# Gated attention in a one-core decoder block: another column order, level products in halves, value products in quarters

## The chip, the cores and the metric

The kernel runs on one core of a Trainium2 chip. The metric is the device time of one execution in microseconds (us), lower is better. The kernel before takes 565.12 us, the median of three runs (565.05 to 565.92).

In this text PE is the matrix engine (TensorE), PEld its weight loads, DVE the vector engine, ACT the scalar engine, POOL the engine GpSimd, and SP the engine that issues most transfers. A matmul has a stationary operand, loaded first, and a moving operand that streams through it column by column; the profile gives each a record of its own. A product of plain float32 operands appears as two pairs of such records.

## The reference

One decoder layer on 512 tokens of width 1024: RMSNorm, one input projection whose columns go to three head groups, an output projection with a residual, an MLP with squared ReLU, and a final RMSNorm. Group A is dilated attention (6 heads), group C block attention (6 heads), and group B, which the change is mainly about, is gated linear attention with 4 heads, keys of 32 and values of 64 columns:

```python
log_a = jax.nn.log_sigmoid((a_lr @ w_a2 + b_a)) / B_GATE_TAU      # per token and key column
b = jnp.cumsum(log_a)                                             # within a chunk
decay = jnp.exp(where(causal, b_i - b_j, NEG_INF))
attn = jnp.einsum('bhnic,bhnjc,bhnijc->bhnij', qc, kc, decay)
o_intra = jnp.einsum('bhnij,bhnjv->bhniv', attn, vc)
o_inter = jnp.einsum('bhnic,bhncv->bhniv', qc * jnp.exp(b), s_prev)
o = rmsnorm(o_intra + o_inter) * norm_w * silu(r)
```

Groups A and C end in a softmax over scores plus bias, `p = exp(l - max) / sum`, followed by the product with the values.

## The kernel before

**Group B without large exponents.** The tokens are cut into four blocks of 128 (`NB`). Inside a block the causal triangle is split by levels, `LEVELS = (64, 32, 16, 8, 4, 2, 1)`: a pair (query i, key j) belongs to the level L at which i lies in the upper half and j in the lower half of the same group of 2L tokens. `levels` makes for each level one tile `kq` (four heads of 32 key columns on the 128 partitions, 512 tokens along the row) in which the lower halves hold keys and the upper halves hold queries, both scaled by the decay to the middle of the group. The level product of block n and head h is then one matmul: all 128 tokens of the block as the stationary operand, the 64 tokens of the upper halves as the moving one, over the head's 32 partitions. The result, 128 keys by 64 queries, goes to the bank `lp[h]` of PSUM. There are 7 levels, 4 blocks and 4 heads, so 112 matmuls; levels are done in pairs (64 and 32, 16 and 8, 4 and 2, 1), and a pair takes four banks, two of tag `s` and two of tag `pt`. The four heads lie in four strips of 32 rows of the PE.

**Merging.** The results are put together in `attn[h]` (128 keys, 4 blocks, 128 queries; zeroed first by POOL). For L of 64 and 32, ACT copies the rectangles. For L of 16 and less, DVE copies the whole result under the mask `lmask` (`copy_predicated`), 256 elements a row for each of 4 heads; queries stand in their natural order, so that a level writes runs of L elements with gaps of L. A bank is given back after the second level of the pair is merged from it.

**Values.** `carry` makes the states between blocks (`smk`) and the decayed queries (`eq`). Then, block by block, one matmul adds the state's part (`eq` by `smk`, 256 columns, not for block 0), and four add `attn[h]` (128 by 128, stationary) by the head's values (64 columns), into the banks `op_`. DVE adds the diagonal part and the result is normalized and gated.

**Softmax.** `attention` goes through six pairs of heads; for each pair and each of four query blocks it spawns two streams `softmax`, one for each head (`side` e = 0, 1). A stream is: DVE adds the bias and takes the minimum `mn` (signs are turned), ACT takes the exponential and the row sum `z`, DVE takes the reciprocal `rz`, and DVE or ACT, whichever would be done first, scales the row. There are 48 such streams. `turn` then transposes the scaled rows on the PE, and `values` multiplies.

**What sets the order.** Every engine runs its instructions in the order in which they were issued. That order is made by `Plan`, which simulates the engines when the program is built: each piece of work is a stream (a generator), and `Plan.run` always issues the step that could start first by its own clock, with a priority as the tie-break. An operation is booked at the cost that `Op.__init__` gives it, and 0.2 us (`SWITCH`) when the matmul before it had another shape class (32 or 64 rows, 32 or 64 columns of the PE). So a changed cost, or an operation more or less, can change the order of everything issued after it. Most lines of the trace bear line 133, where `issue` makes the instruction; the tiles' names tell the work apart: `lp` level products, `attn` merges, `op` value products, `rz`, `z` and `P` softmax, `sps` scores, `ptp` transposes, `po` products of attention with values, `vps`, `qkps`, `ops`, `f1*`, `f2*` the dense projections, `wh` and `wl` the two parts into which ACT and DVE split each weight.

## Time and profile before

| what | us |
|---|---|
| median of three runs | 565.12 |
| the profiled execution | 566.03 |
| its span, first to last instruction | 564.0 |
| PE busy | 553.6 |
| DVE busy | 479.6 |
| ACT busy | 370.3 |
| POOL busy | 69.0 |

The profiled execution is one of its own: its span is 2.03 us shorter than its time, and its time is 0.91 us above the median of the three runs. A group row gives engine, operation, output and inputs, size and count, then the busy time and the mean length of one in ns. A timeline row gives start, length over all of its merged instructions, engine, operation and count. A window row gives the busy time of PE, PEld, DVE, ACT and POOL with the number of instructions, then the granted PE clock and the transfers' share.

### The profile page before, as it was taken

The numbers are of one execution on the slowest core, as the hardware profiler recorded it, in microseconds if no ns is written. First come the engines' busy times: TensorE is split into PE (matmuls) and PEld (weight loads), VectorE is DVE, ScalarE is ACT, GpSimd is POOL, SyncE is SP. The second block draws the span as 40 slices with busy tenths as digits, with TensorE's granted clock in tenths as the row PEclk, the third lists the DMA queues.
The fourth block names the chain that finished last, engine by engine and source line by source line (L and its number), as shares of the span: only waits on it lengthen the run. The fifth ranks groups of instructions, "written<-read, shape, count | busy, mean of one in ns | idle before, by whom it ended". The sixth has DMA issues, their size and how long they took to land.

```text
span 564.0 us, 9463 instructions
## 1 busy us (share of the span) xinstructions
PE 553.6 (98%) x3513; PEld 477.8 (85%) x3513; DVE 479.6 (85%) x874; ACT 370.3 (66%) x659; POOL 69.0 (12%) x90
## 2 busy tenths in 40 slices
PE   8999999999999999999999999999999999999995
PEld 7977887786876768899987899988999888999884
DVE  5799899978867988999799995799957799867985
ACT  5755744694865775989766476855477655579553
POOL 5003110000010002110111010120020110011103
PEclk9999999999999999999999999999999999999998
DMA  8945594685134765992989429687378594395803
GB/s 301 400 121 118 91 261 95 205 320 112 37 43 121 254 146 112 268 274 60 278 212 209 158 64 279 198 149 206 113 162 279 121 201 160 94 216 113 150 18 131
DMA packets 29948, 96.58 MB, mean 171 GB/s; under 512 B 3648, under 2 KB 3690, under 8 KB 29904
## 3 DMA queue, kind: packets, MB, share of 16 engines
q0 software_dynamic: 9456, 33.53, 33.4%
q1 hardware_dynamic: 20160, 62.20, 30.9%
q8 instruction: 27, 0.44, 0.3%
q10 hardware_dynamic: 288, 0.27, 0.1%
q14 instruction: 17, 0.14, 0.1%
HBM read 93.86 MB, written 2.13 MB: 170 GB/s over the span
## 4 chain that ended last, share of the span: by engine, by line
PE 83%; DVE 9%; DMA 3%; ACT 2%; issue 2%; SPq 0%; DVEq 0%; ACTq 0%; POOLq 0%
PE f2X L133 14%; PE f1X L133 13%; PE qkps L133 10%; PE f1Z L133 8%; PE f2Z L133 7%; PE ops L133 7%; PE vps L133 5%; PE f1Y L133 4%; PE f2Y L133 3%; DMA wraw<-in_w 3%; PE ptp L133 3%; PE po L133 2%; DVE wl L133 2%; PE sps L133 2%; PE av L133 1%
## 5 line engine op out<-in xcount | busy, mean ns | idle before, releaser
L133 DVE TENSOR_TENSOR wl<-wraw,wh 128x1024 fp32r<-128x1024 f32 (+2 forms) x174 | 192.0, 1110 | 39.5 <-ACT wh L133 39.1
L133 ACT ACTIVATE wh<-wraw 128x1024 fp32r<-128x1024 f32 (+2 forms) x173 | 164.6, 966 | 58.1 <-DMA wraw<-in_w 12.3
L133 PE MATMUL f1X<-yp,wh 128*128 128x256 f32 x512 | 92.7, 283 | 0.0
L133 PEld LDWEIGHTS f1X<-yp,wh 128*128 128x128 f32 x512 | 80.1, 192 | 0.3
L133 POOL DMA_DIRECT2D wraw<-in_w x46 | 40.5, 948 | 270.2 <-DVE wl L133 227.2
L133 PE MATMUL f1X<-yp,wl 128*128 128x256 f32 x256 | 72.5, 283 | 0.0
L133 PE MATMUL f2X<-wh,Al 128*128 128x512 f32 (+1 forms) x132 | 50.6, 383 | 0.0
L133 PE MATMUL f2X<-wh,Ah 128*128 128x512 f32 (+1 forms) x132 | 50.6, 383 | 0.0
L133 PE MATMUL f2X<-wl,Ah 128*128 128x512 f32 (+1 forms) x132 | 50.5, 383 | 0.0
L133 PEld LDWEIGHTS f1X<-yp,wl 128*128 128x128 f32 x256 | 49.1, 192 | 0.1
L133 PE MATMUL f1Z<-yp,wh 128*128 128x256 f32 x256 | 46.3, 283 | 0.0
L133 ACT ACTIVATE h<-h 128x512 f32<-128x512 f32 x56 | 34.7, 625 | 10.5 <-DVE h L133 9.9
L133 PE MATMUL qkps<-xh,wh 128*128 128x512 f32 x96 | 40.1, 418 | 0.0
L133 PEld LDWEIGHTS f1Z<-yp,wh 128*128 128x128 f32 x256 | 39.9, 192 | 0.0
L133 ACT ACTIVATE P<-P,mn 128x512 f32<-128x512 f32 (+3 forms) x48 | 26.5, 555 | 18.8 <-DVE mn L133 18.8
L133 ACT ACTIVATE Ah<-h 128x512 fp32r<-128x512 f32 x40 | 24.0, 620 | 21.5 <-DVE h L133 21.5
L133 PE MATMUL qkps<-xh,wl 128*128 128x512 f32 x96 | 37.6, 392 | 0.0
L133 PE MATMUL qkps<-xl,wh 128*128 128x512 f32 x96 | 37.5, 390 | 0.0
L133 PE MATMUL f1Z<-yp,wl 128*128 128x256 f32 x128 | 36.2, 283 | 0.0
L133 DVE TENSOR_TENSOR Al<-h,Ah 128x512 fp32r<-128x512 f32 x40 | 26.9, 686 | 3.2 <-ACT Ah L133 3.1
L133 PEld LDWEIGHTS f2X<-wl,Ah 128*128 128x128 f32 x132 | 24.8, 188 | 4.9
L133 PEld LDWEIGHTS f2X<-wh,Ah 128*128 128x128 f32 x132 | 24.8, 188 | 4.8
(264 smaller groups left out, 1220.8 us busy)
## 6 DMA issues: line engine op xcount, KB each, us to landing
wraw<-in_w SPq DMA_DIRECT2D x66, 512.0 KB, 5.2
wraw<-in_w POOLq DMA_DIRECT2D x46, 512.0 KB, 6.7
wraw<-in_wqk SPq DMA_DIRECT2D x12, 512.0 KB, 6.0
wraw<-in_wv SPq DMA_DIRECT2D x10, 512.0 KB, 6.7
wraw<-in_wv POOLq DMA_DIRECT2D x8, 512.0 KB, 5.4
wraw<-in_wo SPq DMA_DIRECT2D x8, 512.0 KB, 7.1
wraw<-in_wo POOLq DMA_DIRECT2D x8, 512.0 KB, 5.5
nb<-tab SPq DMA_DIRECT2D x12, 256.0 KB, 3.5
```

The source lines that it names most:

```text
L133: getattr(getattr(self.nc, op.eng), op.method)(*op.args, **op.kw)
```

## The change

Five edits, all in the diff. (1) The columns of `lp` and `attn` get another order: query i of a block stands at place 4·(i mod 32) + (i div 32). The mask follows. A level then writes runs of 4L elements. To deliver its columns in that order, the moving operand of a level product is read with a step of 32 tokens in its innermost dimension for all levels but 32. (2) Each level product becomes two, one for keys 0 to 63 and one for keys 64 to 127: 224 matmuls with 64 stationary columns. (3) Each value product becomes four with 32 stationary columns, one for each 32 queries; in `attn` these are every fourth element. The three products with the states come first. (4) Level 16 is merged by ACT in four rectangles a head, no longer by DVE; levels 64 and 32 write other places. (5) The two softmax streams of a pair share a tile `z` of two columns; one of them takes both reciprocals in one operation once both sums are there, so neither row is scaled before that. Beside that the planner books level products at 0.024 us each (0.031 before), float32 products by another formula, and 0.2 us more for a float32 product of 512 columns.

```diff
--- before.py
+++ after.py
@@ -58,9 +58,9 @@
             if method != "matmul":
                 self.cost = 0.109
             elif wide and inner[-1].shape[0] == 32:
-                self.cost = 0.031
+                self.cost = 0.024
             elif wide:
-                self.cost = 0.002 + max(n / 600 / (1 + (args[0].shape[0] == 64)), 0.21)
+                self.cost = 0.002 + max(n / 600, 0.21 if args[0].shape[0] > 64 else 0.132) / {32: 4, 64: 2}.get(args[0].shape[0], 1) + 0.2 * (n == 512 and args[0].shape[0] == 128)
             elif inner[-1].shape[0] == 64:
                 self.cost = max(n / 2260, 0.12) / 2
             else:
@@ -820,25 +820,42 @@
             for i, (li, L) in enumerate(pair):
                 kq = lev.pop(li)
                 for n in range(NB):
-                    for h in range(4):
-                        c = kq[32 * h:32 * h + 32, n * 128:(n + 1) * 128]
-                        o = lp[h][:, i * 256 + n * 64:i * 256 + (n + 1) * 64]
-                        ops.append(PE.matmul(o.rearrange("p (m l) -> p m l", l=L), c,
-                                             c.rearrange("p (m l) -> p m l", l=2 * L)[:, :, L:], start=True, stop=True))
+                    for rows in (slice(0, 64), slice(64, 128)):
+                        for h in range(4):
+                            c = kq[32 * h:32 * h + 32, n * 128:(n + 1) * 128]
+                            o = lp[h][rows, i * 256 + n * 64:i * 256 + (n + 1) * 64]
+                            if L == 32:
+                                o = o.rearrange("p (m l) -> p m l", l=L)
+                                d = c.rearrange("p (m l) -> p m l", l=2 * L)[:, :, L:]
+                            elif L == 64:
+                                o = o.rearrange("p (l k) -> p l k", k=2)
+                                d = c[:, L:].rearrange("p (k l) -> p l k", k=2)
+                            else:
+                                o = o.rearrange("p (m l k) -> p m l k", l=L, k=4)
+                                d = c.rearrange("p (k m l) -> p m l k", k=4, l=2 * L)[:, :, L:]
+                            ops.append(PE.matmul(o, c[:, rows], d, start=True, stop=True))
             yield ops
             for i, (li, L) in enumerate(pair):
                 give("lev")
-                m = 64 // L
-                mk = lmask[:, li, :].rearrange("p (m l) -> p m l", l=L)[:, None, :, :].to_broadcast([128, NB, m, L])
+                m = 16 // L
+                mk = lmask[:, li, :].rearrange("p (m l) -> p m l", l=64 if L > 16 else 4 * L)
                 for h, r in enumerate(("s", "s", "pt", "pt")):
-                    o4 = attn[h].rearrange("p n (m l) -> p n m l", l=2 * L)[:, :, :, L:]
-                    src = lp[h][:, i * 256:i * 256 + 256].rearrange("p (n m l) -> p n m l", n=NB, l=L)
-                    if L >= 32:
-                        for j in range(m):
-                            rows = slice(2 * L * j, 2 * L * j + L)
-                            yield ACT.activation(o4[rows, :, j], src[rows, :, j], AF.Copy)
+                    src = lp[h][:, i * 256:i * 256 + 256].rearrange("p (n c) -> p n c", n=NB)
+                    o4 = attn[h].rearrange("p n (l k) -> p n l k", k=4)
+                    if L == 64:
+                        yield ACT.activation(o4[:64, :, :, 2:], src[:64].rearrange("p n (l k) -> p n l k", k=2), AF.Copy)
+                    elif L == 32:
+                        for j in range(2):
+                            rows = slice(64 * j, 64 * j + 32)
+                            yield ACT.activation(o4[rows, :, :, 2 * j + 1], src[rows, :, 32 * j:32 * j + 32], AF.Copy)
+                    elif L >= 16:
+                        for j in range(4):
+                            rows = slice(32 * j, 32 * j + 16)
+                            yield ACT.activation(o4[rows, :, 16:, j], src[rows].rearrange("p n (l k) -> p n l k", k=4)[:, :, :, j], AF.Copy)
                     else:
-                        yield DVE.copy_predicated(o4, mk, src)
+                        o4 = attn[h].rearrange("p n (m l) -> p n m l", l=8 * L)[:, :, :, 4 * L:]
+                        yield DVE.copy_predicated(o4, mk[:, None, :, :].to_broadcast([128, NB, m, 4 * L]),
+                                                  src.rearrange("p n (m l) -> p n m l", l=4 * L))
                     if li == pair[-1][0]:
                         give(r)
         fire("attn")
@@ -849,13 +866,15 @@
         for i in range(2):
             yield ("take", "pt")
             op_.append(bank("pt", "op"))
+        for n in range(1, NB):
+            ops.append(PE.matmul(op_[n // 2][:, n % 2 * 256:n % 2 * 256 + 256], eq[:, n * 128:(n + 1) * 128], smk[n - 1],
+                                 start=n < 3, stop=False, skip_group_check=True))
         for n in range(NB):
-            o = op_[n // 2][:, n % 2 * 256:n % 2 * 256 + 256]
-            vb = vB[n // 2][:, n % 2, :]
-            if n:
-                ops.append(PE.matmul(o, eq[:, n * 128:(n + 1) * 128], smk[n - 1], start=True, stop=False, skip_group_check=True))
-            ops.extend(PE.matmul(o[:, h * 64:(h + 1) * 64], attn[h][:, n, :], vb[:, h * 64:(h + 1) * 64],
-                                 start=(n == 0 and h == 0), stop=h == 3, skip_group_check=True) for h in range(4))
+            for h in range(4):
+                for k in range(4):
+                    ops.append(PE.matmul(op_[n // 2][32 * k:32 * k + 32, n % 2 * 256 + h * 64:n % 2 * 256 + (h + 1) * 64],
+                                         attn[h][:, n, k::4], vB[n // 2][:, n % 2, h * 64:(h + 1) * 64],
+                                         start=False, stop=h == 3, skip_group_check=True))
         yield ops
         for i in range(2):
             yield DVE.tensor_tensor(oB[i].rearrange("p t c -> p (t c)"), op_[i], dv[i].rearrange("p t c -> p (t c)"), op=OP.add)
@@ -1051,12 +1070,24 @@
                 spawn(mix_out(p if p < 3 else p + 2, po, r), 1)
 
     def softmax(P, s, nb, key, last):
-        mn, z, rz = (small(x, (128, 1)) for x in ("mn", "z", "rz"))
+        mn = small("mn", (128, 1))
+        p, side, qb = key
+        if ("z", p, qb) not in st:
+            st["z", p, qb] = small("z", (128, 2)), small("rz", (128, 2))
+        z, rz = st["z", p, qb]
         yield DVE.tensor_tensor_reduce(P, s, nb, 1.0, 3e38, OP.add, OP.min, mn)
         if last:
             give(last)
-        yield ACT.activation(P, P, AF.Exp, bias=mn, scale=-1.0, accum_out=z)
-        yield DVE.reciprocal(rz, z)
+        yield ACT.activation(P, P, AF.Exp, bias=mn, scale=-1.0, accum_out=z[:, side:side + 1])
+        fire(("z", *key))
+        yield ("wait", ("z", p, 1 - side, qb))
+        if ("z", p, qb) in st:
+            st.pop(("z", p, qb))
+            yield DVE.reciprocal(rz, z)
+            fire(("rz", p, qb))
+        else:
+            yield ("wait", ("rz", p, qb))
+        rz = rz[:, side:side + 1]
         yield Any(DVE.tensor_scalar(P, P, rz, None, op0=OP.mult), ACT.activation(P, P, AF.Copy, scale=rz),
                   late=dict(vector=LN))
         fire(key)
@@ -1718,7 +1749,7 @@
     cst[p, 1024 + p // 32] = 1.0
     lm = np.zeros((128, len(LEVELS), 64), np.int32)
     for li, L in enumerate(LEVELS):
-        i = np.array([x for x in range(128) if x // L % 2 == 1])
+        i = np.array([x for x in np.arange(128).reshape(4, 32).T.flat if x // L % 2 == 1])
         j = np.arange(128)
         lm[:, li, :] = (j[:, None] // L % 2 == 0) & (j[:, None] // (2 * L) == i[None, :] // (2 * L))
     return oh, ind, cst, lm
```

## The prediction

> **What bounds the kernel now.** I read the page's busy line first, then the busy time by stage, then the waits of PE.
>
> ```profile
> PE 553.6 (98%) x3513; PEld 477.8 (85%) x3513; DVE 479.6 (85%) x874; ACT 370.3 (66%) x659; POOL 69.0 (12%) x90
> ...
> core 0: us, PE busy (x) PEld busy (x) DVE busy (x) ACT busy (x) POOL busy (x), PEclk, DMA share, GB/s
> 60.00:70.00 10.00, 10.00 (x106) 8.43 (x105) 8.35 (x20) 8.15 (x19) 1.20 (x2) 1.00 0.46 70
> 70.00:80.00 10.00, 10.00 (x100) 8.27 (x100) 10.00 (x25) 3.22 (x4) 1.61 (x2) 1.00 0.99 265
> 90.00:100.00 10.00, 10.00 (x78) 7.78 (x77) 10.00 (x21) 2.19 (x3) 0.00 (x0) 1.00 0.21 68
> 100.00:110.00 10.00, 9.51 (x63) 7.66 (x63) 10.00 (x40) 7.04 (x20) 0.00 (x0) 1.00 0.54 161
> 300.00:557.00 257.00, 257.00 (x1620) 233.92 (x1618) 217.37 (x272) 159.76 (x221) 32.39 (x35) 1.00 0.63 159
> ...
> 0.00:10.00 10.00, 7.62 (x41) 6.99 (x42) 3.82 (x11) 4.82 (x8) 7.04 (x19) 1.00 0.82 277
> 556.00:564.10 8.10, 1.21 (x11) 1.00 (x9) 3.28 (x14) 2.35 (x5) 0.43 (x1) 0.80 0.35 129
> ```
>
> PE is idle 10.4 us of the span: 2.4 us in the first ten, 6.9 us after 556, and some 1.1 us between. So the time is PE's work plus its fixed ends. DVE is as full as PE from 70 to 110 us, where the gated attention runs; after 300 us PE never idles, and nothing of the change lies there. What PE waits for in between:
>
> ```profile
> PE f2Z L133 <- ACT wh L133: 0.4, 1, 0.4
> PE ptp L133 <- DVE P L133: 0.3, 1, 0.3
> PE sps L133 <- DVE mn L133: 0.2, 1, 0.2
> ```
>
> Time saved on PE is therefore worth its full size; time saved on DVE is worth the half microsecond that `ptp` and `sps` wait for it.
>
> **Level products in halves.** One pair of levels, and the last level:
>
> ```profile
> 56.87 2.01 PE L133 MATMUL lp<-kq 32*128 32x64 f32 x64
> 58.81 0.50 PE L133 MATMUL vps<-wh,xh 128*128 128x512 f32 x1
> ...
> 90.41 1.35 PE L133 MATMUL lp<-kq 32*128 32x64 f32 x32
> 91.69 0.50 PE L133 MATMUL vps<-wh,xsh 128*128 128x512 f32 x1
> ```
>
> From start to next start a pair takes 1.94 us for 64 records (two a matmul), the last level 1.28 us for 32. All seven: 3·1.94 + 1.28 = 7.1 us. What sets the price of a record?
>
> ```profile
> 62.00 0.95 PE L133 MATMUL ktp<-hsel,qk 128*128 128x4 f32 x8
> 62.81 0.47 PE L133 MATMUL vps<-wh,xh 128*128 128x512 f32 x1
> ...
> 98.45 1.00 PE L133 MATMUL op<-vB,attn 128*128 128x64 f32 x8
> 99.28 0.65 PE L133 MATMUL op<-m,eq 128*128 128x256 f32 x2
> 99.77 1.00 PE L133 MATMUL op<-vB,attn 128*128 128x64 f32 x8
> ...
> 102.42 1.00 PE L133 MATMUL op<-vB,attn 128*128 128x64 f32 x8
> 103.35 0.44 PE L133 MATMUL sps<-k,q 64*128 64x384 f32 x2
> ```
>
> Eight records with 4 moving columns take 0.81 us (0.10 each), eight with 64 take 0.83 (0.104): the load of 128 stationary columns sets it. In `lp` four heads stand side by side, so 16 groups of four at 0.104 make 1.66 of a pair's 1.94 us; the other 0.28 is the change of shape. In all 56·0.104 + 4·0.28 = 6.9, near the 7.1 measured.
>
> Afterwards there are 448 records with 64 columns, eight of which could stand side by side. That halves share the PE so is shown by
>
> ```profile
> 125.86 4.53 PE L133 MATMUL po<-th,v 128*64 128x256 f32 x32
> 130.31 0.50 PE L133 MATMUL qkps<-xh,wh 128*128 128x512 f32 x1
> ```
>
> (32 records of 64-column halves: by the loop 2·2·2·(512+384+256+128) = 10,240 columns in 4.45 us, 0.43 ns each, where `op<-m,eq` above, 128 wide, needs 0.49 us for 512 columns, 0.96 ns.) Best case: 56 groups of eight at half of 0.104, 2.9 us, plus 1.1 for the changes, 4.0: 2.9 us saved. Against it stands the moving operand, which for six of seven levels now takes every 32nd element. PE has no such row; DVE's merges have:
>
> ```profile
> 68.02 0.43 DVE L133 COPY_PREDICATED attn<-lmask,lp 128x256 f32<-128x256 int32 x1
> 71.49 1.10 DVE L133 COPY_PREDICATED attn<-lmask,lp 128x256 f32<-128x256 int32 x3
> 74.95 1.43 DVE L133 COPY_PREDICATED attn<-lmask,lp 128x256 f32<-128x256 int32 x4
> 78.89 2.05 DVE L133 COPY_PREDICATED attn<-lmask,lp 128x256 f32<-128x256 int32 x5
> 82.37 0.73 DVE L133 COPY_PREDICATED attn<-lmask,lp 128x256 f32<-128x256 int32 x1
> ...
> 92.11 2.48 DVE L133 COPY_PREDICATED attn<-lmask,lp 128x256 f32<-128x256 int32 x4
> ```
>
> Level 8 writes runs of eight (1.43/4 = 0.36 us), level 1 single elements (2.48/4 = 0.62): 0.26 us more over 256 elements, 1.0 ns each. On 64 moving columns that is 0.065 us. But PE reads every second element for level 1 today, and its group of four takes (1.28 − 0.28)/8 = 0.125, at most 0.02 over the rest. Between DVE's full extra and the third of it that PE's own row allows at step two I take about half: 0.056 + 0.035 = 0.09 a group for six levels. 48·0.09 + 8·0.056 + 1.1 = 5.9, **1.0 us saved**. Worst case: no row has records faster than 1.94/64 = 0.03 us; 448 of these are 13.4, 6.3 us lost.
>
> [...]
>
> **Value products in quarters.** 32 records now take 0.83 + 0.84 + 0.83 + 0.93 = 3.4 us. Then 128, four side by side: a load of 32 columns is a quarter of 0.104 = 0.026, with single elements of `attn` 0.032 more by DVE's 1.0 ns; 64 moving columns 0.056; so 32 groups at 0.06 = 1.9. One more change of shape, 0.3. **1.2 us saved.** Bounds: 1.5 saved, or, if only two stand side by side as in `po`, 64·0.06 = 3.8 and 0.7 lost. The state products, now first, wait for the last state:
>
> ```profile
> 98.32 0.43 DVE L133 TENSOR_TENSOR s2m<-s2m,cst 128x256 f32<-128x256 f32 x1
> ```
>
> It ends at 98.75, and PE began at 98.45: 0.3 us if nothing moved. I take 0, for DVE gets there earlier.
>
> **Merges.** DVE loses four merges of level 16 (0.43 + 1.10) and the short runs: level 1 goes from 0.62 to 0.36 each, level 2, the last of the x5 row (2.05 − 4·0.36 = 0.6) and three singles like that at 82.37 (some 0.55 from start to start, less than the 0.73 recorded), gets runs of eight in place of two and saves 0.2 each. 1.5 + 1.0 + 0.8 = 3.3 us of DVE's full stretch. That frees the 0.5 us that PE waits for DVE; I count **0.4**. ACT gains 16 copies, each smaller than
>
> ```profile
> L133 ACT ACTIVATE attn<-lp 32x128 f32<-32x128 f32 x8 | 2.1, 265 | 0.1
> ```
>
> so under 4.2 us, in a stretch (70 to 80 us) where it is busy 3.2 of 10. Its other 12 copies now write with gaps; at DVE's 1.0 ns that is 4·0.26 + 8·0.13 = 2.1 us more. Both lie beside dense products on PE and cost nothing; without that cover the next levels' banks would come up to 6 us late, and `vps` on PE would have to fill it as it does now.
>
> The end of the merges also lets `attention` start, and with it, on SP's queue,
>
> ```profile
> 98.30 7.13 SPq L133 DMA_DIRECT2D nb<-tab  x4
> ```
>
> No transfer is added, but these would be issued up to 3 us earlier, ahead of weight loads that stand there now. PE waits for no transfer in the list above, so I take 0; if that cover were gone, a weight would come later by the four tiles' own landing, the 7.1 us of this row at most.
>
> **One reciprocal per pair.**
>
> ```profile
> 99.39 0.72 ACT L133 ACTIVATE P<-P,mn 128x512 f32<-128x512 f32 x1 [6.10 <-DVE mn L133]
> ...
> 100.66 0.72 ACT L133 ACTIVATE P<-P,mn 128x512 f32<-128x512 f32 x1 [0.45 <-DVE mn L133]
> ...
> 100.80 0.49 DVE L133 TENSOR_SCALAR P<-P,rz 128x512 f32<-128x512 f32 x1
> ...
> 109.71 0.28 DVE L133 RECIPROCAL rz<-z 128x1 f32<-128x1 f32 x3
> ```
>
> 24 fewer of 48, at some 0.09 us each, free 2.2 us of DVE between 100 and 201 us. The first row of a pair, scaled at 100.80 today, must now wait for the second exponential, until about 101.5: 0.7 us later. Behind the waiting reciprocal DVE's next steps stand, the weight splits among them, and the transposes wait for the rows; the second row was their last one anyway and PE has `vps` and `qkps`. I take 0: what DVE's freed time can gain is in the 0.4 above, and 0.7 can be lost.
>
> **The planner's order** is made anew from the first level product on. Of the 1.1 us of idle PE no more can be won; a loss has no bound. I take 0 and widen by 1.
>
> **The sum** is made against the profiled execution: 566.03 − 1.0 − 1.2 − 0.4 = 563.4. That execution lies 0.91 above the runs' median, so for the median 565.12 − 2.6 = **562.5 us**.
>
> **Rivals.** *Better:* steps cost PE nothing. Level products 4.0 us; 2.9 + 1.2 + 0.4 = 4.5 saved, 560.6. For it: level 1 today. Against it: DVE's rows.
>
> *Hidden:* PE is cheaper, but waits for what DVE delivers, which was just as full up to 110 us; or the new order and the paired wait give 2 us back. 564.0 to 566.2. For it: DVE 10.00 of 10. Against it: DVE loses over 3 us itself.
>
> *Slower, the halves take turns:* both halves of a head read the same 32 partitions in steps; if they cannot be served together, a group of eight is twice 0.09. 48·0.18 + 8·0.056 + 1.1 = 10.2, 3.3 lost; less 1.2 and 0.4, 1.7 lost: 566.8. It decides from a group price of 0.145 us, where level products lose 1.6 (48·0.145 + 1.5 = 8.5). Against it: `po` reads the same partitions from two halves without loss, though in order.
>
> *Slower, records have a floor:* PE can take in no more than one record per 0.03 us, the fastest row here. Level products 13.4, values 128·0.03 = 3.8 plus 0.3: 6.3 + 0.7 − 0.4 = 6.6 lost, 571.7. For it: four times the records in the values, twice in the levels. Against it: the 0.03 is explained by loads.
>
> [...]
>
> **Chances.** Forecast 0.45, better 0.12, hidden 0.18, turns 0.15, floor 0.10. A measurement of this kernel can tell about 0.2%, 1.1 us, from no change. Faster: 0.43 + 0.12 + 0.02 = 0.57; same: 0.02 + 0.14 + 0.02 = 0.18; slower: 0.02 + 0.13 + 0.10 = 0.25. The range from 560.0 to 567.5 leaves out the floor and the edges of its neighbours, 0.16; the forecast's own is 561.0 to 564.0.
>
> **What would show it.** In the profile after: the span of an `lp` group of 128 records (1.0 to 1.7 us right; 2.6 and more, turns; 3.5 and more, floor), and whether level 32 alone is faster; 128 `op` records in about 1.9 us; 16 merges on DVE, none above 0.45 us; 24 `rz`; PE idle between 10 and 556 us at or below 1.1 us. The forecast is wrong if PE's waits grow past 2 us, or if level products take over 8.5.

## The result and the profile after

The changed kernel takes 573.51 us (median; 572.41 to 575.36) where the kernel before takes 565.52 beside it (565.05 to 566.69): a ratio of 1.0149, 95% interval 1.0134 to 1.0164. It is **slower by 8 us**, and the time lies above the forecast of 562.5 and above the range up to 567.5. The profiled execution took 572.84 us.

The busy time by stage (columns as in the prediction; the last row is the whole middle of the run):

```profile
core 0: us, PE busy (x) PEld busy (x) DVE busy (x) ACT busy (x) POOL busy (x), PEclk, DMA share, GB/s
65.00:70.00 5.00, 3.88 (x109) 2.72 (x112) 4.32 (x10) 4.54 (x11) 0.86 (x1) 0.96 0.57 96
70.00:75.00 5.00, 5.00 (x58) 4.04 (x47) 2.32 (x9) 4.12 (x15) 0.87 (x1) 0.70 0.48 155
75.00:80.00 5.00, 5.00 (x73) 3.92 (x74) 4.81 (x11) 3.52 (x6) 0.00 (x0) 1.00 1.01 253
80.00:85.00 5.00, 1.64 (x92) 1.29 (x77) 0.61 (x1) 0.00 (x0) 0.86 (x1) 0.83 1.01 236
85.00:90.00 5.00, 5.00 (x17) 3.94 (x13) 3.81 (x9) 2.48 (x3) 0.00 (x0) 0.50 0.52 107
...
10.00:556.00 546.00, 540.37 (x3741) 464.16 (x3740) 461.42 (x804) 370.55 (x661) 57.57 (x68) 0.99 0.64 168
```

Two of these rows in the kernel before:

```profile
85.00:90.00 5.00, 5.00 (x24) 4.20 (x23) 5.00 (x10) 4.87 (x9) 0.00 (x0) 1.00 0.71 141
10.00:556.00 546.00, 544.75 (x3465) 469.85 (x3465) 472.54 (x851) 363.15 (x647) 61.48 (x72) 1.00 0.65 170
```

Before, PE idled 1.25 us between 10 and 556 by this row (1.1 by the prediction's count); now it is 546 − 540.4 = 5.6 us, most of it in two places, around 67 and around 82. Behind each the granted clock falls: 0.70 from 70 to 75, 0.50 from 85 to 90, where before it was 1.00. Both places lie in level products. The timeline of PE (start, duration, what ended the idle time before):

```profile
58.49 1.64 PE L133 MATMUL lp<-kq 32*64 32x64 f32 x128
60.06 0.33 PE L133 MATMUL ktp<-cst,ek 128*128 128x128 f32 x1
...
66.23 0.41 PE L133 MATMUL lp<-kq 32*64 32x64 f32 x2
66.97 0.41 PE L133 MATMUL lp<-kq 32*64 32x64 f32 x2 [0.32 <-ACT attn L133]
67.78 0.41 PE L133 MATMUL lp<-kq 32*64 32x64 f32 x2 [0.40 <-ACT attn L133]
68.59 2.14 PE L133 MATMUL lp<-kq 32*64 32x64 f32 x122 [0.40 <-ACT attn L133]
70.66 0.80 PE L133 MATMUL vps<-wh,xh 128*128 128x512 f32 x1
...
78.81 2.36 PE L133 MATMUL lp<-kq 32*64 32x64 f32 x116
84.54 0.51 PE L133 MATMUL lp<-kq 32*64 32x64 f32 x12 [3.36 <-issue]
84.98 0.80 PE L133 MATMUL vps<-wh,xsh 128*128 128x512 f32 x1
...
113.38 2.22 PE L133 MATMUL op<-vB,attn 128*32 128x64 f32 x128
115.53 0.86 PE L133 MATMUL sps<-k,q 64*128 64x384 f32 x8
```

The first pair runs as predicted: 128 records in 60.06 − 58.49 = 1.57 us. The second gets its four banks one by one until 68.59, from ScalarE. The third stops after 116 of its 128 records for 3.36 us, and no engine is named: `issue` is time in which PE waits for nothing that the profile shows. Behind the stop, as behind the second pair, the same dense product takes 0.80 us instead of the 0.39 to 0.50 where the clock is 1.00. The waits of PE say the same in sum:

```profile
PE lp L133 <- issue: 3.4, 1, 3.4
PE lp L133 <- ACT attn L133: 1.1, 3, 0.4
```

ScalarE's timeline ahead of the second pair:

```profile
62.98 1.06 ACT L133 ACTIVATE wh<-wraw 128x1024 fp32r<-128x1024 f32 x1
63.95 0.62 ACT L133 ACTIVATE e<-e 128x512 f32<-128x512 f32 x1
64.59 0.69 ACT L133 ACTIVATE v<-vps,rstd 128x512 f32<-128x512 f32 x1
65.17 1.05 ACT L133 ACTIVATE wh<-wraw 128x1024 fp32r<-128x1024 f32 x1
66.12 2.42 ACT L133 ACTIVATE attn<-lp 32x128 f32<-32x128 f32 x6
```

Six merges of level 32 that free the banks come behind 3.1 us of other work, and each takes 0.40 us (2.42/6; 0.265 before). What the prediction named for `attn` and `rz` (operation, count: duration in ns, shortest/median/longest):

```profile
L133 ACT ACTIVATE attn<-lp x28: 271/282/403, 60.2 to 75.5; 16x64 f32<-16x64 f32 x16, 32x128 f32<-32x128 f32 x8, 64x256 f32<-64x256 f32 x4
L133 DVE COPY_PREDICATED attn<-lmask,lp x16: 425/431/451, 76.3 to 94.6; 128x256 f32<-128x256 int32 x16
...
L133 DVE RECIPROCAL rz<-z x24: 144/159/167, 105.0 to 208.7; 128x2 f32<-128x2 f32 x24
```

### The profile page after: what moved, and what is told of

Read it like the earlier page. It is cut to its first block, busy times and chain, and to the rows that moved or that the text cites. A ratio compares the mean times of both kernels' runs of the same rounds, so it can differ in the third digit from the quotient of the medians.

```text
span 571.0 us, 10099 instructions
## 1 busy us (share of the span) xinstructions
PE 557.2 (98%) x3833; PEld 479.1 (84%) x3833; DVE 473.8 (83%) x840; ACT 380.5 (67%) x681; POOL 68.9 (12%) x90
## 4 chain that ended last, share of the span: by engine, by line
PE 83%; DVE 10%; ACT 3%; issue 2%; DMA 1%; SPq 0%; ACTq 0%; DVEq 0%
PE f1X L133 16%; PE f2X L133 15%; PE f1Z L133 8%; PE qkps L133 8%; PE f2Z L133 8%; PE ops L133 7%; PE f1Y L133 4%; PE f2Y L133 4%; PE vps L133 3%; DVE wl L133 2%; PE po L133 2%; PE ptp L133 2%; PE av L133 1%; DVE P L133 1%; PE sps L133 1%
## 5 line engine op out<-in xcount | busy, mean ns | idle before, releaser
L133 ACT ACTIVATE wh<-wraw 128x1024 fp32r<-128x1024 f32 (+2 forms) x173 | 164.5, 966 | 59.6 <-DMA wraw<-in_w 17.1
```

The costliest lines, as they stand in the source:

```text
L133: getattr(getattr(self.nc, op.eng), op.method)(*op.args, **op.kw)
```

## The experiments

**Theory 1**: the stop in the third pair is a wait for PE's own instructions. Its rival at first: a bank or an operand that comes late at that place (theory 2). In the diffs, `op.real` is what is issued in place of an operation that the planner books as ever; so the order of all engines stays that of the kernel it is made from. Kernels named a_ are made from the changed kernel, b_ from the one before.

**a_whole**, the changed kernel with whole level products:

```diff
...
+                            ops[-1].real = [PE.matmul(full, c, d, start=True, stop=True)] if rows.start == 0 else []
```

(`full` is the whole product's place in `lp[h]`.)

> The changed kernel with its level products undivided again (64 records a pair instead of 128, 128 stationary columns each); the order of every engine's instructions is that of the changed kernel, and nothing else differs. Theory 1 (instructions come late): PE's stop of 3.6 us inside the third pair is a wait for its own instructions, of which the halves use up twice as many in the same time. Then the stop is gone here, the clock between 85 and 90 us is 1.00 instead of 0.50, a pair takes 1.9 us, and the time falls from 573.5 to about 569 us. Theory 2 (a bank or an operand comes late at that place of the order): the stop of 3 to 4 us stays between the same two products, and the time is 574 to 575 us, as the undivided pairs cost 0.4 us more each.

Measured: 567.42 us, ratio to before 1.0042 (1.0022 to 1.0062). With whole products 573.5 − 567.4 = **6.1 of the 8 us** are gone. The stop is gone and the clock stays up:

```profile
80.00:85.00 5.00, 5.00 (x68) 4.31 (x62) 4.21 (x9) 2.04 (x3) 0.87 (x1) 1.00 1.00 270
85.00:90.00 5.00, 5.00 (x50) 3.91 (x48) 5.00 (x12) 2.83 (x5) 0.87 (x1) 1.00 0.91 160
```

A late bank at that place of the order would have stayed. In the changed kernel's profile the parts are the stop (3.4), the half clock from 85 to 90 (5 · 0.50 = 2.5) and from 70 to 75 (5 · 0.30 = 1.5), less about 1 us that the halves save: 6.4. This is an estimate and no full account: the medians differ by 6.1, but the two profiled executions by 5.2; the fall from 70 to 75 also comes without halves (a_whole16, below); and the third pair of a_whole takes 3.3 us (78.25 to 81.51) instead of the 1.94 before, with no wait named.

**a_shift64 and a_shift144**, the changed kernel with 16 and 36 tiny products at the very start:

```diff
+        for _ in range(16):
+            nc.tensor.matmul(warm[:32, :2], ones[:, :32], ones[:, :2], start=True, stop=True)
```

> The changed kernel with 16 tiny products (32 stationary columns, 2 moving) after the nine that warm the clock, before the first load has landed; 64 more instructions of PE ahead of everything, all orders else the same. PE stopped in the third pair after record 116 of 128, which is after a multiple of 256 instructions. Theory 1 (instructions come late, in packets of 256): the boundary lies 32 records earlier, at record 84, and the packet is asked for some 7 us earlier, as more dense products lie behind it. The stop moves away from record 116 and shrinks to 1 us or nothing, and the time is 568 to 570 us. Theory 2 (a wait for a bank or an operand): the stop stays after record 116 at 3.6 us, and the time is 573 to 574 us.

> The same with 36 tiny products, 144 instructions of PE. Theory 1: the boundary lies at record 44 of the third pair, the packet behind it was asked for before the pair began, and the stop is gone or moved to record 44; 568 to 570 us. If another boundary now falls into the second pair (between 66 and 71 us), it may stop there instead. Theory 2: a stop of 3.6 us after record 116 as before, 573 to 574 us.

Measured: 571.91 us (ratio 1.0124, 1.0098 to 1.0150) and 571.93 (1.0120, 1.0101 to 1.0139). With 64 instructions more the third pair runs through, and the **second** stops, in the timeline of a_shift64:

```profile
68.90 2.04 PE L133 MATMUL lp<-kq 32*64 32x64 f32 x111 [0.40 <-ACT attn L133]
73.97 0.51 PE L133 MATMUL lp<-kq 32*64 32x64 f32 x11 [3.03 <-issue]
74.40 0.80 PE L133 MATMUL vps<-wh,xh 128*128 128x512 f32 x1
...
83.60 2.13 PE L133 MATMUL lp<-kq 32*64 32x64 f32 x128
85.66 0.50 PE L133 MATMUL vps<-wh,xsh 128*128 128x512 f32 x1
```

The expectation had the time wrong (568 to 570), because it did not see that the boundary before moves into the second pair. That the stop goes where the count sends it speaks for theory 1 all the more. The count of PE's products and loads from the start to the end of the stop, in the changed kernel:

```profile
0.00:84.50 84.50, 78.63 (x727) 65.46 (x728) 66.81 (x132) 54.24 (x101) 16.27 (x32) 0.97 0.72 211
```

and in a_shift64:

```profile
0.00:73.90 73.90, 68.75 (x602) 57.91 (x602) 61.64 (x121) 47.01 (x81) 15.16 (x31) 0.97 0.68 207
```

727 + 728, with 18 semaphore and drain instructions that the trace has and this view leaves out, are 1473; 602 + 602 + 13 are 1217. The difference is 256; the expectation puts the stop at a multiple of it, which these counts are not (both leave 193), so it is the difference that the runs show. In a_shift144 no pair stops (the third takes 2.5 us from 82.3), but the tiny products cost more than I thought: they take 2.4 us, the clock reads 0.83 from 5 to 15 us, and the first pair begins at 61.99 us instead of 58.49. Less these 3.5 us the time would be 568.4, inside theory 1's range.

What 256 is can be read from the page of the changed kernel (queue: packets, MB, share of the engines' time):

```profile
q8 instruction: 30, 0.49, 0.3%
```

An estimate, if this queue carries PE's instructions alone, which is not shown: 0.49 MB over 2 · 3833 products and loads are 64 bytes each, and over 30 packets 16 KB each: 256 instructions, the difference above. The trace agrees in the count, one packet for each boundary: with boundaries counted from the 1473rd instruction in steps of 256, the kernel before passes them at 59.4, 74.4 and 90.4 us, and packets start at 59.6, 73.0 and 91.6, within 1.4 us of each passing. When a packet is asked for, and how long ahead of its use it has to land, the profile does not show; 73.0 is 1.4 us ahead of PE's own passing. Before, 256 instructions last some 15 us; the 128 records of a pair are 256 instructions in 1.6 to 2.5 us.

**b_halves**, the kernel before with halves and nothing else (columns in their old order):

```diff
...
+                        for r in (0, 1):
+                            group.insert(r * (h + 1) + h, PE.matmul(o[64 * r:64 * r + 64].rearrange("p (m l) -> p m l", l=L), c[:, 64 * r:64 * r + 64],
+                                         c.rearrange("p (m l) -> p m l", l=2 * L)[:, :, L:], start=True, stop=True))
```

> The kernel before, with its level products in halves and nothing else changed: columns in their old order, the order of every engine's instructions that of before. Theory 1 (PE stops because its instructions come late): by the count of PE's instructions the third pair lies as in the changed kernel, the boundary of a packet again at record 116 of 128, and the weight loads fill the DMA engines in that stretch as they do there. A pair that isn't stopped takes 1.6 us instead of 1.94, 1.3 us saved over all levels; the third pair stops for 2 to 4 us and the clock falls behind it; 566.5 to 569 us. Rival (the stop needs the changed kernel's order, or its reads with a step of 32 elements): no stop, 564.2 us.

> The kernel before with its level products in halves once more, for one profile. Its twelve runs fell into two groups, 563.4 to 565.3 us and 568.2 to 569.7 us, and the profile was one of the first group, without a stop. Theory 1: if this run is one of the second group, its profile has the stop of 3 to 4 us inside the third pair and a lower clock behind it; if it is one of the first, it has neither. Rival (the two groups differ elsewhere): the third pair takes 1.8 us in a run of either group.

Measured: a median of 566.76 us (ratio 1.0022, 0.9995 to 1.0049) that says little, for the twelve runs are two groups: six from 563.42 to 565.33, six from 568.19 to 569.69. The profile is of the first (563.42):

```profile
75.19 1.84 PE L134 MATMUL lp<-kq 32*64 32x64 f32 x128
76.97 0.50 PE L134 MATMUL vps<-wh,xsh 128*128 128x512 f32 x1
```

The same kernel's second profile, b_halves_again, took 570.35 us:

```profile
75.02 1.76 PE L134 MATMUL lp<-kq 32*64 32x64 f32 x116
81.63 0.51 PE L134 MATMUL lp<-kq 32*64 32x64 f32 x12 [4.85 <-issue]
82.07 0.80 PE L134 MATMUL vps<-wh,xsh 128*128 128x512 f32 x1
```

One program, the same place, the same record 116 (again 727 products and 728 loads). The lower six runs have a median of 564.1 us and the upper six one of 569.3, against 565.25 before; if their profiles stand for the groups, the halves save some 1.2 us with the packet in time and lose 4 without. In the first profile the packet starts at 73.0 us, ahead of the pair; in the second at 79.4, when PE already stands. So neither the new order nor the step of 32 elements is needed for the stop.

**a_packed32**, the changed kernel with ScalarE's level 32 written in runs:

```diff
-                            yield ACT.activation(o4[rows, :, :, 2 * j + 1], src[rows, :, 32 * j:32 * j + 32], AF.Copy)
+                            yield ACT.activation(attn[h][rows, :, 64 * j + 32:64 * j + 64], src[rows, :, 32 * j:32 * j + 32], AF.Copy)
```

> The changed kernel, with ScalarE's eight merges of level 32 written in one run of 32 instead of every fourth element. They land in other places, so that part of the gated attention is not the reference's; work and order are the same. Theory A (the gaps in the writes made the merges slow, and the second pair waits for its banks through them): a merge takes 0.27 us instead of 0.40, the wait of the second pair at 66 to 68.6 us shrinks by some 1.0 us, and the time falls to about 572.5 us. Theory B (the merges come late because ScalarE's queue was ordered anew, not because each is slow): the wait keeps its length within 0.5 us and the time stays at 573 to 574 us. The stop in the third pair is as long as in the changed kernel by either, within what the shorter wait moves it.

Measured: 571.58 us (ratio 1.0115, 1.0097 to 1.0132), 1.9 less than the changed kernel. Its group of merges, that of the changed kernel, and the stretch behind the second pair in a_packed32:

```profile
L133 ACT ACTIVATE attn<-lp 32x128 f32<-32x128 f32 x8 | 2.1, 262 | 0.1
L133 ACT ACTIVATE attn<-lp 32x128 f32<-32x128 f32 x8 | 3.1, 387 | 0.1
```

```profile
70.00:75.00 5.00, 5.00 (x23) 4.10 (x23) 2.39 (x9) 4.75 (x18) 0.86 (x1) 1.00 0.84 247
```

387 ns become 262. The second pair has all its banks at 67.8 instead of 68.6, and the clock does not fall behind it (1.00 instead of 0.70); the stop in the third pair stays (3.9 us). Theory A holds, by more than it said: the gaps in the writes cost about twice what the wait shows. The profiles fit that: 0.8 us of wait and 5 · 0.30 = 1.5 us of half clock, less 0.5 by which this stop is longer, make 1.8.

**b_quarters and b_cols**, the kernel before with quarters alone, and with quarters and the new order of the columns:

```diff
...
+            for h in range(4):
+                for k in range(4):
+                    op = PE.matmul(o[32 * k:32 * k + 32, h * 64:(h + 1) * 64], attn[h][:, n, k::4], vb[:, h * 64:(h + 1) * 64],
+                                   start=(n == 0 and h == 0), stop=h == 3, skip_group_check=True)
...
```

(b_quarters reads 32 columns side by side, `32 * k:32 * k + 32`, in place of `k::4`.)

> The kernel before, with its value products in quarters (128 records of 32 stationary columns instead of 32 of 128) and nothing else changed, columns and orders as before. The prediction's term: 3.4 us become 2.2, 1.2 us saved, 564.3 us (564.0 to 564.8). Rival (PE is held by DVE in that stretch, which is full): the time stays at 565.2 to 565.8 us. By theory 1 no stop is to be seen, since the 192 further instructions come in a stretch where the DMA engines are 0.2 to 0.5 busy.

> The kernel before with the new order of the columns, the merges that follow from it and the value products in quarters; the level products stay whole, level 16 is merged by VectorE and each row has its own reciprocal as before; all orders are those of before. VectorE's merges fall from 0.62 us (level 1) and some 0.55 (level 2) to 0.36 to 0.44; ScalarE's merges of levels 64 and 32 take longer (0.40 instead of 0.27 at level 32). Theory A (the slower merges alone make the second pair wait for its banks): a wait of 0.3 us or more ahead of the second pair, 564.5 to 565.5 us. Theory B (that wait came from ScalarE's new order, in which weight copies stand ahead of the merges): no wait there, and the quarters' 1.2 us are left, 564.0 to 564.4 us.

Measured: 564.44 us (ratio 0.9978, 0.9969 to 0.9988) and 563.89 (0.9973, 0.9962 to 0.9984). The quarters' 1.2 us are there. The new columns add nothing that can be told: VectorE is relieved, but the second pair takes 2.5 us in b_cols instead of 1.94, with a wait of 0.3 us that is named for `kq`, not for the banks. So the time, 0.1 us below theory B's range, speaks for B, and a wait as long as theory A's is there, by another releaser. b_cols is faster than both kernels of this case.

**b_best**, b_cols with halves where they don't meet the third pair:

```diff
...
+                        if L in (4, 2):
+                            continue
...
```

> The new order of the columns and the value products in quarters on the kernel before (as measured at 563.9 us), and in addition the level products of the first two pairs and of the last level in halves; the third pair stays whole, since its instructions would be used up where the DMA engines are full. All orders are those of the kernel before. Theory 1 (instructions late in the third pair alone): a first pair of 1.6 us instead of 1.94, the last level 1.12 or less, no stop, runs close together, 563.0 to 563.6 us. Rival (the halves lose PE's instructions wherever they stand): runs in two groups, some near 563 and some near 568 us.

Measured: 564.09 us (ratio 0.9982, 0.9971 to 0.9992), all runs within 1.5 us. No second group: with the third pair whole, none of eleven runs shows the price of the stop. But the halves bring nothing over b_cols either. The first pair gains 0.37 us, the second still takes 2.5 us and the last level 1.1, as in b_cols; where the gain goes then, the runs do not show.

**b_recip**, the kernel before with one reciprocal per pair (the change's `softmax`):

> The kernel before with one reciprocal per pair of rows and nothing else changed; the planner's order from there on is made anew. Theory A (the prediction: nothing on the path): 565.0 to 566.0 us. Theory B (the pairing makes the transposes wait, as three waits of 0.4 to 0.6 us for the row maxima's chain show between 120 and 210 us in the changed kernel, which the kernel before does not have): those waits are here too, 566.3 to 567.2 us.

Measured: 566.03 us (ratio 1.0011, 1.0002 to 1.0020): 0.1 to 1.1 us slower, between the ranges of the two theories. The order made anew is part of that. The waits are those of theory B, where the kernel before has 0.2 at `sps` and 0.3 (for VectorE) at `ptp`:

```profile
PE sps L133 <- DVE mn L133: 0.7, 2, 0.4
PE ptp L133 <- ACT th L133: 0.5, 1, 0.5
```

**b_costs and b_act16**, the planner's new costs alone, and b_cols with level 16 on ScalarE:

```diff
+                    elif L >= 16:
+                        for j in range(4):
+                            rows = slice(32 * j, 32 * j + 16)
+                            yield ACT.activation(o4[rows, :, 16:, j], src[rows].rearrange("p n (l k) -> p n l k", k=4)[:, :, :, j], AF.Copy)
```

> The kernel before with the planner's new costs alone; every instruction is one of before, but their order is made anew. Theory A (the new order of ScalarE's queue comes from the costs): weight copies stand ahead of the last merges of levels 64 and 32, the second pair waits for its banks by some 1 to 2 us, and the time is 566 to 567.5 us. Theory B (it comes from the new merges themselves): no wait ahead of the second pair, 565.0 to 565.8 us.

> The new order of the columns and the quarters on the kernel before, level products whole, and level 16 merged by ScalarE as in the changed kernel; costs are those of before, the order from there on is made anew. Theory A (the prediction: these copies lie beside dense products and cost nothing): 563.5 to 564.4 us, as with VectorE's merges (563.9). Theory B (16 copies of 0.28 us ahead of the weight copies in ScalarE's queue make PE wait): waits of 0.5 us or more between 65 and 85 us and 565 to 566.5 us.

Measured: 565.11 us (ratio 1.0001, 0.9993 to 1.0010) and 567.04 (1.0036, 1.0022 to 1.0051). The costs put weight copies ahead of the merges, as expected, and yet the time is that of before: theory A falls there. Level 16 on ScalarE looked like 3 us over b_cols, more than theory B said. Half a microsecond of it, the third pair in b_act16:

```profile
75.99 0.48 PE L133 MATMUL lp<-kq 32*128 32x64 f32 x6
77.00 2.05 PE L133 MATMUL lp<-kq 32*128 32x64 f32 x58 [0.53 <-DVE attn L133]
```

**a_whole16** takes the same 16 copies away from a_whole:

```diff
-                    elif L >= 16:
-                        for j in range(4):
-                            rows = slice(32 * j, 32 * j + 16)
-                            yield ACT.activation(o4[rows, :, 16:, j], src[rows].rearrange("p n (l k) -> p n l k", k=4)[:, :, :, j], AF.Copy)
```

> The changed kernel with undivided level products (567.4 us) and level 16 merged by VectorE again; the order of PE's products is the same until 80 us, ScalarE's queue is that of the changed kernel without its 16 copies. Theory A (the copies cost: the third pair waits for the banks that they free): 564.3 to 566 us. Theory B (the 3 us that the copies seemed to cost on the kernel before came with the order made anew there): 566.8 to 568 us.

Measured: 567.91 us (ratio 1.0041, 1.0025 to 1.0057), no better than a_whole. But its runs are two groups as well, 565.71 and 566.06, and six from 567.81 to 569.21; the profile is of the second, and shows why:

```profile
70.00:75.00 5.00, 5.00 (x38) 4.21 (x35) 3.29 (x10) 1.00 (x2) 0.86 (x1) 0.50 0.42 132
75.00:80.00 5.00, 5.00 (x21) 4.02 (x20) 3.00 (x6) 0.90 (x2) 0.00 (x0) 0.84 1.03 247
```

Behind a wait of the second pair as long as in a_whole (0.7 us in sum in both) the clock fell here and not there. 5 · 0.50 + 5 · 0.16 = 3.3 us go that way, more than the copies could be worth. The two shorter runs, whose mean clock is 0.997 (the six have 0.992 to 0.994), lie 1.5 us below the median of a_whole (0.995 to 0.998), in favour of theory A, but they are only two. So what level 16 on ScalarE costs is **not settled**: between nothing (the medians of this pair) and 3 us (b_act16, whose order was made anew).

**Why is the packet late?** Theory 1a: it waits behind weight transfers; theory 1b: it is asked for too late, whatever the engines carry. In the kernel before, a packet started within 1.4 us of each of three passings. In the changed kernel PE passes the boundary ahead of the stop at 76.5 us. From there to 82.2 the queues carry no packet of instructions, and the engines are full with two others (59.7 + 44.0%):

```profile
q1 hardware_dynamic: 339, 1.13, 59.7%
q0 software_dynamic: 135, 0.49, 44.0%
```

It lands at 83.2. But full engines are not the whole reason. In b_halves they are 0.98 busy from 70 to 75 us, about as in b_halves_again (1.05), and the packet is in time. And in a_shift64 PE passes the boundary ahead of its stop at 63.9 us, the engines then carry next to nothing (0.01) for 3 us, and yet the packet starts only at 71.8:

```profile
63.94:67.00 3.06, 2.99 (x14) 2.06 (x12) 2.62 (x5) 3.02 (x6) 0.86 (x1) 1.00 0.01 3
```

**a_light and b_halves_light** narrow the accumulating loads:

```diff
-        yield POOL.dma_start(t, wv_d[q[1], 2 * q[0] + ip], accum_op=OP.add)
+        op = POOL.dma_start(t, wv_d[q[1], 2 * q[0] + ip], accum_op=OP.add)
+        op.real = [POOL.dma_start(t[:, :32], wv_d[q[1], 2 * q[0] + ip][:, :32], accum_op=OP.add)]
+        yield op
```

> The changed kernel with its accumulating weight loads (GpSimd's queue) narrowed from 1024 to 32 columns, so that sums of weights are left out and the output isn't the reference's; all orders are those of the changed kernel. The DMA engines' busy share between 75 and 85 us falls from 1.01 to about 0.6. Theory 1a (the packet of instructions waits behind weight transfers): no stop in the third pair, full clock from 85 to 90 us, 567 to 569 us. Theory 1b (the packet is asked for too late, whatever the engines carry): the stop stays at 3 to 4 us and the time at 572.5 to 574 us.

> The kernel before with its level products in halves and its accumulating weight loads narrowed in the same way (sums of weights are left out). Theory 1a: all runs lie in the lower group, 563 to 565.3 us. Theory 1b: two groups as with the full loads, or all runs in the upper one, 568 to 570 us.

Measured: 573.14 us (ratio 1.0148, 1.0134 to 1.0163), stop of 3.6 us; and 562.98 to 568.79 us (ratio 1.0021, 1.0001 to 1.0041), still spread over both groups, with a stop of 3.0 us in the profile (567.48). By the expectations' words this is theory 1b; but the plain loads still kept the engines 0.6 busy there, and nearly full for stretches. **a_light2 and b_halves_light2** narrow these too:

```diff
+            if key[0] == "qk" and pieces.index((key, src, n)) > [k for k, *_ in pieces].index("v"):
+                op.real = [POOL.memset(raw[:, 32:], 0.0), SP.dma_start(raw[:, :32], src[:, :32])]
...
+                if n in (4, 5):
+                    op.real = [POOL.memset(t[:, 32:], 0.0), SP.dma_start(t[:, :32], wv_d[q[1], 2 * q[0] + ip][:, :32])]
```

> The changed kernel with its accumulating weight loads and the plain weight loads issued between 66 and 82 us narrowed from 1024 to 32 columns (GpSimd fills the rest with zeros), so that most of these weights are left out and the output isn't the reference's; all orders else are those of the changed kernel. The DMA engines' busy share between 70 and 82 us falls below 0.4. Theory 1a (the packet waits behind transfers): the packet starts before the third pair or early in it, no stop, 567 to 570 us. Theory 1b (the packet is asked for too late, whatever the engines carry): the stop stays at 3 us or more, 572 to 574 us.

> The kernel before with its level products in halves and the same loads narrowed. Theory 1a: all runs in the lower group, 562.5 to 565 us. Theory 1b: two groups as before, the upper from 566.5 to 569.7 us.

> The same kernel as the one with both kinds of loads narrowed, for one more profile. If it takes 571 us or more: by theory 1b the stop is there, in the third pair or the second, with the DMA engines below 0.2 busy in the five us before the packet starts; by theory 1a there is no stop, and the time is lost to a halved clock alone. If it takes 567 us, it shows neither.

Measured: a_light2 took 566.76 us in the profiled run, and 571.80 to 572.58 in three others (ratio of the four 1.0102, 1.0068 to 1.0136); its second profile 566.49. b_halves_light2 lies between 564.00 and 568.39 (ratio 1.0015, 0.9999 to 1.0030). In the profile of a_light2 the engines are nearly idle, and the packet comes between 73.3 and 75 us:

```profile
70.00:75.00 5.00, 5.00 (x58) 4.06 (x49) 2.31 (x9) 4.10 (x15) 1.26 (x2) 0.69 0.04 7
```

```profile
q8 instruction: 1, 0.02, 5.0%
```

8 to 9 us earlier than in the changed kernel, with no stop; so in both profiles of this kernel. With free engines the packet can be early; that is for theory 1a. The three runs near 572 us have no profile, and the second profile did not fall among them. But their spans and mean clocks are known: 569.9 to 570.6 us at 0.990 to 0.994, where the profiled run has 564.9 us at 0.994. An estimate from these figures: at 0.990 the lower clock costs 570.5 · 0.010 = 5.7 us at most, in the profiled run 564.9 · 0.006 = 3.4, so it explains about 2.3 of 5.6 us, and in the run at 0.994 next to nothing. In the rest of the time PE must have stood or waited, which theory 1a did not expect. That it was the same stop is likely but not shown, and what delays the packet stays **open**.

## Why the prediction was wrong, step by step

- **Level products in halves** is the step that failed. It counted 1.0 us saved; the halves cost about 6.1. The size of PE's own work came out, partly by luck: in b_halves without a stop the four groups take 1.53 + 1.53 + 1.78 + 1.22 = 6.1 us by their starts, and 5.9 were forecast. But b_halves has no step of 32, and without one the prediction's price was 0.056 a group of eight, 56 · 0.056 + 1.1 = 4.2. With the step nothing is added: in the changed kernel's first pair the 64 records of level 64 (step 32) and the 64 of level 32 (in order) each take 0.71 us, 0.089 a group. So a group is dearer than was said, the step free, and the two errors cancel. Halves do share PE: 128 records take 1.57 us where 64 whole ones took 1.94. What the step left out is that a record is also two instructions, a product and a load, and that a stop moved with their count (1473 and 1217): it costed PE's work and never what feeds it. The runs show a stop of 3.0 to 4.9 us there, and 2.5 us of half clock behind it. The worst case of 6.3 us was the right size by the wrong mechanism; the rival of a floor came nearest (571.7) and is refuted, for the first pair runs at 1.57/128 = 12 ns a record.
- **The clock** was not in the sum at all. It read 1.00 in the stages before, and every wait was priced at its own length; here 3.4 us of stop drew 2.5 us of half clock behind it.
- **The merges.** On VectorE as forecast: 16, 425 to 451 ns. On ScalarE the forecast of 1.0 ns an element was right (0.265 to 0.39 us for 128). That they "lie beside dense products on PE and cost nothing" was wrong: the second pair waited for its banks from 66.2 to 68.6. The prediction priced the loss of that cover at up to 6 us and then took 0; a_packed32 shows 1.9 us from the gaps alone, and the six merges also came late, behind 3.1 us of other work in the order made anew.
- **Value products in quarters** was right: 2.15 us, where 1.9 and 0.3 for a change of shape were forecast, and 1.2 us saved by b_quarters (0.7 to 1.8) as forecast.
- **The 0.4 us from VectorE** cannot be told apart in b_cols; no run shows this gain.
- **One reciprocal per pair**, taken as 0 with 0.7 to be lost, costs 0.1 to 1.1 us in b_recip, with the order that it makes.
- **The planner's order**, taken as 0: new costs alone change nothing (b_costs). What the order that all five edits make together costs, no run shows by itself.
- Of the list of what would show it, the `lp` group, the merges and the 24 reciprocals came out; the last item, PE's idle time, decided: 5.6 us instead of at most 1.1.

The parts do not add up in full. The halves carry about 6.1 of the 8 us, the stop and what follows it. Of the other 1.9 the quarters give back 1.2 and the reciprocals take some 0.6, and the 2.5 that are left lie between the slower merges on ScalarE, level 16, the order made anew and a clock that falls in some runs.

## What to carry to other kernels

Cutting a product into pieces that run side by side can be cheap on TensorE and still lose: here a pair of levels fell from 1.94 to 1.57 us, and the 256 instructions of the third such pair met a stop of 3.4 us. Count the instructions that a burst uses up, and look for `issue` idle time that no semaphore explains. Where runs of one kernel fall into two groups, take a second profile before believing the median. Price a stall of TensorE with the clock that falls behind it (here 2.5 us behind 3.4), not with its length alone.

## What the hardware showed that I had not expected

PE stops at the same count (727 products and 728 loads) in five of these kernels, and 256 instructions earlier in a_shift64, for 3.0 to 4.9 us. In the changed kernel, b_halves_again and a_shift64 a packet starts only after PE has stopped (at 82.2, 79.4 and 71.8 us); that PE's instructions come in packets of 256 is the estimate from the page of the changed kernel (30 packets for 7666 instructions) and this difference. The packet itself took under 1 us on its queue in the changed kernel (82.2 to 83.2), but PE went on only 1.4 us after it had landed.

The granted clock fell behind stops, and behind less. In b_halves_again PE stands from 76.78 to 81.63 us, and from 80.96 to 87.79 the clock is 0.50 (0.60 in the mean from 80 to 85, 0.72 from 85 to 90). In the changed kernel the clock is 0.50 from 83.28 us, where PE had stood only since 81.17, and from 69.63 to 73.04, behind the waits of the second pair, none of them over 0.4 us. In a_shift144 it is 0.50 from 8.29 to 11.71, behind tiny products, with PE busy 5.00 of the 5 us around. And it is not the same each time: behind the second pair it was 0.50 from 69.78 to 76.61 in a_whole16 and 1.00 in a_whole, whose waits for the banks sum to the same 0.7 us. What decides it is not shown.

Small records that stand side by side start 12 ns apart on average (1.57 us for the 128 of the first pair), and a moving operand with a step of 32 elements costs PE nothing that shows (0.71 us for 64 records with or without it), while writes with a step of four cost ScalarE 1.0 ns for each element (387 ns instead of 262 for 128).
